# High parts of the weights moved to byte 96, loads in turns, and each half of stationary weights in two runs of four

## The chip, the cores and the metric

The kernel runs on one core of a Trainium2 chip, in one launch. The metric is the device time of that launch in microseconds, the median of several runs. All weights come from the chip's memory (HBM) once, some 317 MB, and are used once.

## The reference

The reference is two layers of an encoder over 256 positions of 2048 channels, in fp32, and a last RMSNorm. Each layer is a norm, one wide input projection, a mixer per group of heads, SiLU gates, one output projection of 4096 channels back to 2048, and the residual.

```
h = rms_norm(x, norm_w[0])                                   # layer 0
a_q, a_i, a_ff, a_fb, a_g, b_u, b_g = split(h @ w_in)        # 2048 -> 7 x 2048
a_out = hgrn2(a_q, a_i, a_ff, a_fb) * silu(a_g)              # gated linear recurrence, both directions
b_out = fourier(b_u) * silu(b_g)                             # 2-D DFT per group, linear map
x = x + concat(a_out, b_out) @ w_out
h = rms_norm(x, norm_w[1])                                   # layer 1
c_in, c_b, c_c, c_g, d_z, d_xbc, d_dt = split(h @ w_in)      # 2048 -> 13376
c_out = c_b * conv3(c_c * c_in) * silu(c_g)
d_out = ssd(d_xbc, d_dt, d_z)                                # scan in chunks, both directions
x = x + concat(c_out, d_out) @ w_out
return rms_norm(x, final_norm_w)
```

## The kernel before

Each fp32 operand is split into a high part (the value as TensorE's type fp32r holds it) and a low part (what is left). A product is then three products: high by high, high by low, low by high. TensorE's fp32r matmuls do these. The activations stand in `xx` (layer inputs, 16 blocks of 128 channels, each with its high and its low part of 256 positions behind one another) and in `mm` (inputs of the output projections).

The weights are worked off in halves: 561 tiles of 128 x 1024, in the order of use (`halves`, L105 to L112). SyncE's queue loads a half into one of five raw buffers (`load`, L125). ScalarE rounds it to its high part (L155), VectorE subtracts to get its low part (L156). Both go to a ring of three places (`fetch`, L133), up to four halves ahead of use (`half`, L175). The last eight halves have three more places.

There are three kinds of large matmul:
- Projections by channel (`gemm_half`, L184; 368 halves): the weights are stationary, eight blocks of 128 x 128 per half, and the activations move. Eight matmuls with the high weights take both parts of the activations (512 columns, L187), then eight with the low weights take the high activations (256 columns, L190).
- Token projections (`tokens`, L553, matmuls at L563; names pv and pg): the activations are stationary, the weights move, 512 columns. Twelve matmuls per half, eight with a high part moving and four with a low part.
- Output projections (`tproduct`, L198, matmuls at L206; names o, oC, oD): the inputs in `mm` are stationary, the weights move, 512 columns, twelve per half.

Where a tile begins in its partition is part of the change. Bytes are counted modulo 512 here. All steps between blocks of `xx`, `mm` and the weights are multiples of 512, so a tile has one place. `xx` begins at 480 (96 modulo 128; a spare tile `fx` of 120 floats puts it there), `mm` at 0. The ring's three places are 8704 bytes apart, 17 x 512. In projections and token projections the high part begins at 32 and the low part at 32; in output projections both begin at 0 (`oh, ol`, L146).

Small products (heads of the recurrence, Fourier groups, scan) are put between by `later(n, fn)` (L159): they are due n halves later, and `due` runs what is due before a half is taken, the earliest first and among those of one due time the one entered first. A scheduler then gives each engine its final order within what the tiles allow. The opening is written out at L301: it loads weight halves (w) and blocks of the activations (x) in the order `wxwxwwxwx`; the first weight half comes in two pieces.

Of the kernel before, what the change touches and what calls it, by code (L numbers as in the profile page):

```python
# [9 lines left out]
F32R = mybir.dt.float32r  # L10
# [5 lines left out]
P = 128  # L16
D = 2048
L = 256
# [38 lines left out]
def encoder_kernel(ctx: ExitStack, tc, xT, xN, w_ev, w_evo, w_dt, w_od, w_odo, fw, fnr, par, con, acon, tric, outN):  # L57
    nc = tc.nc
    V, S, PE = nc.vector, nc.scalar, nc.tensor
# [22 lines left out]
    def pcol(name, i):  # L82
        return parT[:, PCOL[name] + i:PCOL[name] + i + 1]
# [9 lines left out]
    def t2(name, shape=(2, L)):  # L93
        return lpool[0].tile([P, *shape], F32, tag="t2", name=name, bufs=N2)
# [16 lines left out]
    DTH = 2 * (112 + 32) + 1  # L111
    halves.insert(DTH, w_dt)  # L112

    moving = set(range(2 * 112, 2 * 144)) | set(range(len(halves) - 64, len(halves)))
    loaded, ready, waiting = {}, {}, []
    state = {"load": 0, "next": 0, "use": 0}
    HK = KT // 2
    NRAW, NHL, AHEAD = 5, 3, 4

    def pieces(n):  # L120
        return (slice(0, 512), slice(512, 1024)) if n == 0 else (slice(0, 1024),)
# [3 lines left out]
    def load():  # L125
        n = state["load"]
        state["load"] = n + 1
        raw = wpool.tile([P, HK * P], F32, tag=f"raw{n % NRAW}", name=f"raw{n}")
        for c in pieces(n):
            nc.sync.dma_start(out=raw[:, c], in_=halves[n][:, c])  # L130
        loaded[n] = raw

    def fetch():  # L133
        n = state["next"]
        state["next"] = n + 1
        if n >= state["load"]:
            load()
        raw = loaded.pop(n)
        kept = n - (len(halves) - 8)
        i = n % NHL if kept < 0 else kept % (2 * NHL)  # L140
        pool = wpool if i < NHL else endp[0]

        ring = i < NHL
        hi = pool.tile([P, HK * P + (8 if ring else 0)], F32R, tag=f"hi{i}", name=f"hi{n}")
        lo = pool.tile([P, HK * P + (120 if ring else 0)], F32R, tag=f"lo{i}", name=f"lo{n}")
        oh, ol = (0, 0) if not ring else (0, 120) if n in moving else (8, 0)  # L146
        hi, lo = hi[:, oh:oh + HK * P], lo[:, ol:ol + HK * P]
        if n == DTH:

            for i, w in enumerate((hi, lo)):  # L150
                w, r = w.rearrange("p (k s c) -> p k s c", s=2, c=64), raw.rearrange("p (i k c) -> p i k c", i=2, c=64)[:, i]
                S.activation(w[:, :, 0], r, AF.Copy)
                V.tensor_tensor(w[:, :, 1], r, w[:, :, 0].bitcast(F32), SUB)
        for c in pieces(n) if n != DTH else ():
            S.activation(hi[:, c], raw[:, c], AF.Copy)  # L155
            V.tensor_tensor(lo[:, c], raw[:, c], hi[:, c].bitcast(F32), SUB)  # L156
        ready[n] = (hi, lo)

    def later(n, fn):  # L159

        waiting.append((state["use"] + n, len(waiting), fn))

    def due(upto):
        while True:
            now = [w for w in waiting if w is not None and w[0] <= upto]
            if not now:
                return
            w = min(now)
            waiting[w[1]] = None
            w[2]()  # L170

    def flush():
        due(1 << 30)

    def half():  # L175

        n = state["use"]
        due(n)
        while state["next"] <= min(n + AHEAD, len(halves) - 1):
            fetch()  # L180
        state["use"] = n + 1
        return ready.pop(n)

    def gemm_half(out, a, k0, first, last):  # L184
        hi, lo = half()
        for k in range(HK):
            PE.matmul(out, lhsT=hi[:, k * P:(k + 1) * P], rhs=a[:, k0 + k].rearrange("p s n -> p (s n)"),  # L187
                      start=(first and k == 0), stop=False)
        for k in range(HK):
            PE.matmul(out[:, :L], lhsT=lo[:, k * P:(k + 1) * P], rhs=a[:, k0 + k, 0], start=False,  # L190
                      stop=(last and k == HK - 1))

    def gemm(out, a):

        for h in range(2):
            gemm_half(out, a, h * HK, h == 0, h == 1)
# [90 lines left out]
        PE.matmul(warm[:, :P], lhsT=ones, rhs=ones, start=True, stop=True)  # L287
    xcs = []

    def x_load():  # L290
        c = len(xcs)
        xc = t2(f"x{c}")
        for k in (slice(0, 1), slice(1, 2)) if c == 0 else (slice(0, 2),):
            nc.sync.dma_start(out=xc[:, k], in_=xT[:, 2 * c + k.start:2 * c + k.stop, :])
        xcs.append(xc)

    def x_split(c):
        for k in range(2):
            split_by(xx[:, 2 * c + k], xcs[c][:, k, :], pcol("nw0", 2 * c + k))

    for n in "wxwxwwxwx":  # L301
        (load if n == "w" else x_load)()
    for k in range(2):
        w, src = pcol("nw0", k), xcs[0][:, k, :]
        V.tensor_scalar(xx[:, k, 0], src, w, None, MUL)  # L305
        if k == 0:
            fetch()
        V.scalar_tensor_tensor(xx[:, k, 1], src, w, xx[:, k, 0].bitcast(F32), MUL, SUB)
    for c in (1, 2):
        fetch()  # L310
        x_split(c)
# [11 lines left out]
    def norm0b():  # L323
# [6 lines left out]
        rs["tok"] = rsqrt("n0t", pt[:, 0:2], 2)  # L330

    later(4, lambda: nc.sync.dma_start(out=parT[:, 16:], in_=par[:, 16:]))
    later(12, norm0)
    later(14, norm0b)


    with lay:
# [33 lines left out]
        def hgrn(h, q, Z, v, sg, vo):  # L371
# [94 lines left out]
                split_by(mm[:, h], pt.rearrange("p i n -> p (i n)"), pcol("hnw", h))  # L466


            later(6, scores)
            later(10 if h % 2 else 12, values)  # L470
            later(12 if h % 2 else 16, norm)

# [80 lines left out]
        def tokens(*names, each=lambda u: None):  # L553

            ps_ = [[pmain(f"{name}_{b}") for b in range(2)] for name in names]
            for u in range(8):
                each(u)
                for p in ps_:
                    hi, lo = half()
                    for k in range(2):  # L560
                        for b in range(2):
                            for n, (s_, w) in enumerate(((0, hi), (0, lo), (1, hi))):
                                PE.matmul(p[b], lhsT=xx[:, 2 * u + k, s_, b * P:(b + 1) * P],  # L563
                                          rhs=w[:, k * 4 * P:(k + 1) * 4 * P], start=(u == 0 and k == 0 and n == 0),
                                          stop=(u == 7 and k == 1 and n == 2))
            due(state["use"])
            return ps_

        def x_on(u):
            if 1 <= u < 6:  # L570
                x_split(u + 2)
            if u < 4:
                x_load()

        nrt = sp.tile([P, 2], F32, tag="nrt", name="nrt")
        for hp in range(8):
# [20 lines left out]
            for i in range(2):  # L597
                h = 2 * hp + i
                q = evac(f"q{h}", proj(f"pq{h}"))
                Z = t2(f"Z{h}")  # L600
                for d in range(2):
                    scaled(Z[:, d, :], f"Z{h}_{d}", proj(f"pz{h}_{d}"), rs[0])
                hgrn(h, q, Z, v, sg, (h % 4) * P)
# [18 lines left out]
    def tok(name, bufs=4):  # L622
        return op.tile([P, 4 * P], F32, tag="tok", name=name, bufs=bufs)
# [10 lines left out]
    for g in range(4):  # L634
# [7 lines left out]
        for b in range(2):  # L642
            V.tensor_tensor(x1[b], x1[b], po[b], ADD)
            nc.sync.dma_start(out=x1d[b, :, g * 4 * P:(g + 1) * 4 * P], in_=x1[b])
            s = tok(f"x1s{g}_{b}", 4)
# [4 lines left out]
    with ExitStack() as lay:  # L650
# [52 lines left out]
        H2 = 64  # L703
        dtp, first_b = pmain("pdt"), pmain("pB0")
        gemm_half(first_b, xx, 0, True, False)
        hl = half()
        due(state["use"])
        for k in range(KT):
            PE.matmul(dtp, lhsT=hl[k // HK][:, k % HK * P:(k % HK + 1) * P], rhs=xx[:, k].rearrange("p s n -> p (s n)"),
                      start=(k == 0), stop=(k == KT - 1))  # L710
        gemm_half(first_b, xx, HK, False, True)
        due(state["use"])
        xd, ee, rr, r2, dt, la, sc, rw = [t1(f"dt_{n}")[:H2] for n in ("x", "e", "r", "r2", "dt", "la", "sc", "rw")]
# [318 lines left out]
```

## Time and profile before

| | us |
|---|---|
| median of 3 runs (range) | 1670.77 (1670.48 to 1671.13) |
| profiled execution | 1671.18 |
| its span | 1669.4 |
| TensorE busy | 1656.1 |
| VectorE busy | 1236.5 |
| ScalarE busy | 935.8 |

The span is the time from the first to the last instruction; the profiled execution's own time also holds what lies around it. The page gives the busy time of each engine, the chain of work that ended last, and groups of instructions by line. Matmuls overlap: one lasts longer in the records than the distance to the next one's start, so their pace is read from starts. The chain of work shows it directly, since there a piece ends where the next one begins.

### The profile page before, as it was taken

How to read it: one execution, taken by the hardware profiler on the slowest of the kernel's cores; microseconds unless marked ns; L12 is line 12 of the kernel's file. 1: busy time of each engine (PE TensorE's matmuls, PEld its weight loads, DVE VectorE, ACT ScalarE, POOL GpSimd, SP SyncE). 2: the span in 40 equal slices, each digit the busy share in tenths (PEclk: the TensorE clock that was granted, in tenths of full speed). 3: DMA queues.
4: the chain of work that ended last, by engine and by line, in shares of the span. 5: the costliest groups of instructions: out<-in, count | busy, mean ns of one | idle time of the engine just before them, and what ended most of it. 6: DMA issues, size and time to landing. Idle time of an engine off the chain costs nothing.

```text
span 1669.4 us, 24942 instructions
## 1 busy us (share of the span) xinstructions
PE 1656.1 (99%) x9350; PEld 1412.3 (85%) x9350; DVE 1236.5 (74%) x2165; ACT 935.8 (56%) x1525; POOL 1.7 (0%) x12
## 2 busy tenths in 40 slices
PE   9999999999999999999999999999999999999997
PEld 7888888888888888888888888888888888888886
DVE  7788658875877589654458998888888798865554
ACT  6566456654665466544445666666655565654443
POOL 0000000000000000000000000000000000000000
PEclk9999999999999999999999999999999999999999
DMA  8654555455544654576665676656656665566553
GB/s 293 213 171 153 182 191 179 156 171 196 174 167 163 195 179 152 165 224 208 202 218 184 208 212 204 198 190 205 199 184 204 194 192 185 178 225 226 191 194 123
DMA packets 98265, 319.07 MB, mean 191 GB/s; under 512 B 11040, under 2 KB 19936, under 8 KB 98016
## 3 DMA queue, kind: packets, MB, share of 16 engines
q1 hardware_dynamic: 97712, 316.95, 57.9%
q8 instruction: 73, 1.20, 0.3%
q10 hardware_dynamic: 432, 0.53, 0.1%
q14 instruction: 48, 0.39, 0.1%
HBM read 313.18 MB, written 4.26 MB: 190 GB/s over the span
## 4 chain that ended last, share of the span: by engine, by line
PE 97%; DVE 1%; DMA 1%; ACT 0%; issue 0%; SPq 0%; DVEq 0%; ACTq 0%
PE pz L187 10%; PE o L206 10%; PE pg L563 5%; PE oC L206 5%; PE oD L206 5%; PE pz L190 5%; PE pv L563 5%; PE pu L187 4%; PE px L187 4%; PE pq L187 4%; PE pbg L187 4%; PE pcg L187 4%; PE pcb L187 3%; PE pci L187 3%; PE pcc L187 3%; PE pbg L190 2%
## 5 line engine op out<-in xcount | busy, mean ns | idle before, releaser
L156 DVE TENSOR_TENSOR lo<-raw,hi 128x1024 fp32r<-128x1024 f32 (+1 forms) x561 | 683.9, 1221 | 382.2 <-ACT hi L155 377.6
L155 ACT ACTIVATE hi<-raw 128x1024 fp32r<-128x1024 f32 (+1 forms) x561 | 594.3, 1060 | 565.1 <-PE o L206 86.0
L187 PE MATMUL pz<-xx,hi 128*128 128x512 f32 x768 | 194.9, 396 | 0.0
L187 PEld LDWEIGHTS pz<-xx,hi 128*128 128x128 f32 x768 | 137.2, 188 | 25.6
L206 PE MATMUL o<-hi,mm 128*128 128x512 f32 x512 | 126.8, 390 | 0.0
L206 PEld LDWEIGHTS o<-hi,mm 128*128 128x128 f32 x512 | 95.8, 188 | 19.7
L190 PEld LDWEIGHTS pz<-xx,lo 128*128 128x128 f32 x768 | 102.0, 188 | 8.7
L190 PE MATMUL pz<-xx,lo 128*128 128x256 f32 x768 | 103.3, 277 | 0.0
L563 PE MATMUL pv<-hi,xx 128*128 128x512 f32 x256 | 83.0, 394 | 0.8 <-DVE xx L305 0.8
L563 PE MATMUL pg<-hi,xx 128*128 128x512 f32 x256 | 81.6, 393 | 0.9 <-ACT hi L155 0.9
L206 PE MATMUL o<-lo,mm 128*128 128x512 f32 x256 | 68.5, 389 | 0.0
L187 PE MATMUL pcb<-xx,hi 128*128 128x512 f32 x256 | 66.4, 401 | 0.0
L187 PE MATMUL px<-xx,hi 128*128 128x512 f32 x256 | 66.0, 400 | 0.0
L187 PE MATMUL pu<-xx,hi 128*128 128x512 f32 x256 | 65.6, 398 | 0.0
L187 PE MATMUL pbg<-xx,hi 128*128 128x512 f32 x256 | 65.5, 398 | 0.0
L187 PE MATMUL pci<-xx,hi 128*128 128x512 f32 x256 | 65.4, 397 | 0.0
L187 PE MATMUL pq<-xx,hi 128*128 128x512 f32 x256 | 65.0, 395 | 0.0
L206 PE MATMUL oC<-hi,mm 128*128 128x512 f32 x256 | 64.7, 390 | 0.2 <-ACT hi L155 0.2
L187 PE MATMUL pcc<-xx,hi 128*128 128x512 f32 x256 | 64.8, 395 | 0.0
L187 PE MATMUL pcg<-xx,hi 128*128 128x512 f32 x256 | 64.8, 395 | 0.0
L206 PE MATMUL oD<-hi,mm 128*128 128x512 f32 x256 | 63.4, 390 | 0.0
L563 PEld LDWEIGHTS pg<-hi,xx 128*128 128x128 f32 x256 | 48.0, 188 | 11.7 <-ACT hi L155 1.3
(560 smaller groups left out, 2781.0 us busy)
## 6 DMA issues: line engine op xcount, KB each, us to landing
raw<-in_w_ev SPq DMA_DIRECT2D x223, 512.0 KB, 4.1
raw<-in_w_od SPq DMA_DIRECT2D x208, 512.0 KB, 4.4
raw<-in_w_evo SPq DMA_DIRECT2D x64, 512.0 KB, 4.0
raw<-in_w_odo SPq DMA_DIRECT2D x64, 512.0 KB, 4.5
ab<-rd SPq DMA_DIRECT2D x64, 128.0 KB, 4.9
fw<-in_fw SPq DMA_DIRECT2D x8, 256.0 KB, 5.7
xr<-in_xN SPq DMA_DIRECT2D x8, 256.0 KB, 5.9
x1d<-xr SPq DMA_DIRECT2D x8, 256.0 KB, 4.9
```

Of the source, the lines that this page charges most:

```text
L155: S.activation(hi[:, c], raw[:, c], AF.Copy)
L156: V.tensor_tensor(lo[:, c], raw[:, c], hi[:, c].bitcast(F32), SUB)
L187: PE.matmul(out, lhsT=hi[:, k * P:(k + 1) * P], rhs=a[:, k0 + k].rearrange("p s n -> p (s n)"), start=(first and k == 0), stop=False)
L190: PE.matmul(out[:, :L], lhsT=lo[:, k * P:(k + 1) * P], rhs=a[:, k0 + k, 0], start=False, stop=(last and k == HK - 1))
L206: PE.matmul(outs[b], lhsT=a[:, k0 + 2 * u + k, s_, b * P:(b + 1) * P], rhs=w2[part][:, k * 4 * P:(k + 1) * 4 * P], start=(u == 0 and part ...
L563: PE.matmul(p[b], lhsT=xx[:, 2 * u + k, s_, b * P:(b + 1) * P], rhs=w[:, k * 4 * P:(k + 1) * 4 * P], start=(u == 0 and k == 0 and n == 0), ...
```

## The change

The diff has four parts.

1. In each ring place the low part is now allocated first and has 8 spare floats, the high part behind it has 120. In the projections by channel the high part begins at 96 modulo 512 (`PLACES`, 16 floats behind a place of 32), the low part stays at 32. In output projections both stay at 0. In token projections (`passing`) the high part begins at 32, 96 or 480 by ring place, the low part at 32.
2. `gemm_half` goes through its eight blocks in two runs: four matmuls with high weights, four with low, four with high, four with low.
3. The two pieces of the first weight half and the two of the first activations are loaded in turns.
4. `later` takes a second key: the scores of every second head go behind whatever else is due at the same half.

```
+    PLACES = (16, 16, 16)
...
+        for i, c in enumerate(pieces(n)):
             nc.sync.dma_start(out=raw[:, c], in_=halves[n][:, c])
+            if n == 0:
+                x_load(i)
...
-        hi = pool.tile([P, HK * P + (8 if ring else 0)], F32R, tag=f"hi{i}", name=f"hi{n}")
-        lo = pool.tile([P, HK * P + (120 if ring else 0)], F32R, tag=f"lo{i}", name=f"lo{n}")
-        oh, ol = (0, 0) if not ring else (0, 120) if n in moving else (8, 0)
+        lo = pool.tile([P, HK * P + (8 if ring else 0)], F32R, tag=f"lo{i}", name=f"lo{n}")
+        hi = pool.tile([P, HK * P + (120 if ring else 0)], F32R, tag=f"hi{i}", name=f"hi{n}")
+        oh, ol = (0, 0) if not ring else (120, 0) if n in moving else ((0, 16, 112)[i] if n in passing else PLACES[i], 8)
...
-    def later(n, fn):
-        waiting.append((state["use"] + n, len(waiting), fn))
+    def later(n, fn, last=0):
+        waiting.append((state["use"] + n, last, len(waiting), fn))
...
-        for k in range(HK):
-            PE.matmul(out, lhsT=hi[:, k * P:(k + 1) * P], rhs=a[:, k0 + k].rearrange("p s n -> p (s n)"),
-                      start=(first and k == 0), stop=False)
-        for k in range(HK):
-            PE.matmul(out[:, :L], lhsT=lo[:, k * P:(k + 1) * P], rhs=a[:, k0 + k, 0], start=False,
-                      stop=(last and k == HK - 1))
+        for ks in (range(HK // 2), range(HK // 2, HK)):
+            for k in ks:
+                PE.matmul(out, lhsT=hi[:, k * P:(k + 1) * P], rhs=a[:, k0 + k].rearrange("p s n -> p (s n)"),
+                          start=(first and k == 0), stop=False)
+            for k in ks:
+                PE.matmul(out[:, :L], lhsT=lo[:, k * P:(k + 1) * P], rhs=a[:, k0 + k, 0], start=False,
+                          stop=(last and k == HK - 1))
...
-            later(6, scores)
+            later(6, scores, h % 2)
```

On TensorE, the projections of the first Fourier group (pu) stand like this before, two of them:

```order
L187 MATMUL pu_0_925<-xx,hi_793 128x512 x8
L190 MATMUL pu_0_925<-xx,lo_794 128x256 x8
L187 MATMUL pu_0_925<-xx,hi_815 128x512 x8
L190 MATMUL pu_0_925<-xx,lo_816 128x256 x8
L187 MATMUL pu_1_994<-xx,hi_842 128x512 x8
```

and now, of one and a half:

```order
L198 MATMUL pu_1_994<-xx,hi_843 128x512 x4
L201 MATMUL pu_1_994<-xx,lo_842 128x256 x4
L198 MATMUL pu_1_994<-xx,hi_843 128x512 x4
L201 MATMUL pu_1_994<-xx,lo_842 128x256 x4
L198 MATMUL pu_1_994<-xx,hi_865 128x512 x4
L201 MATMUL pu_1_994<-xx,lo_864 128x256 x4
```

Each run of eight became two of four, with the low run between them. The output tile and the number of matmuls are the same.

On TensorE, between the two gate projections (pbg) of that group, before (sa and sb are a head's scores, po its values, fp the Fourier products over channels):

```order
L449 MATMUL po_1115<-v_528,ST_947 128x128 x4
L425 MATMUL sa_1128<-DQ_912,D_900 64x64 x2
L425 MATMUL sa_1128<-q_1_917,k_1_918 64x64 x2
L425 MATMUL sa_1128<-DQ_912,D_900 64x64 x4
L425 MATMUL sa_1128<-q_1_917,k_1_918 64x64 x2
L425 MATMUL sa_1128<-DQ_912,D_900 64x64 x2
L431 MATMUL sb_1129<-q_1_919,k_1_920 64x128 x4
L507 MATMUL fp_1152<-acT,F_1055 128x128 x4
L187 MATMUL pbg_1_1114<-xx,hi_997 128x512 x8
```

and now:

```order
L461 MATMUL po_1115<-v_528,ST_947 128x128 x4
L198 MATMUL pbg_1_1114<-xx,hi_998 128x512
L519 MATMUL fp_1128<-acT,F_1055 128x128
L437 MATMUL sa_1136<-DQ_912,D_900 64x64
L519 MATMUL fp_1128<-acT,F_1055 128x128 x3
L437 MATMUL sa_1136<-DQ_912,D_900 64x64
L437 MATMUL sa_1136<-q_1_917,k_1_918 64x64 x2
L437 MATMUL sa_1136<-DQ_912,D_900 64x64 x4
L437 MATMUL sa_1136<-q_1_917,k_1_918 64x64 x2
L437 MATMUL sa_1136<-DQ_912,D_900 64x64 x2
L443 MATMUL sb_1137<-q_1_919,k_1_920 64x128 x4
L198 MATMUL pbg_1_1114<-xx,hi_998 128x512 x3
```

One large matmul moved up behind the values, and the Fourier products went ahead of or between the first scores; all the same instructions are there. The same happens in six groups.

On SyncE's queue, the opening before (raw is a weight half or a piece of one, x a block of activations):

```order
L130 DMA raw_102<-in_w_ev 128x512 x2
L294 DMA x_105<-in_xT 128x256 x2
L130 DMA raw_108<-in_w_ev 128x1024
L294 DMA x_110<-in_xT 128x512
L130 DMA raw_112<-in_w_ev 128x1024
L130 DMA raw_114<-in_w_ev 128x1024
L294 DMA x_116<-in_xT 128x512
```

and now:

```order
L138 DMA raw_102<-in_w_ev 128x512
L305 DMA x_104<-in_xT 128x256
L138 DMA raw_102<-in_w_ev 128x512
L305 DMA x_104<-in_xT 128x256
L138 DMA raw_108<-in_w_ev 128x1024
L305 DMA x_110<-in_xT 128x512
L138 DMA raw_112<-in_w_ev 128x1024
L138 DMA raw_114<-in_w_ev 128x1024
```

The first two transfers of each kind stand in turns; from the second weight half on the order is the same.

## Rows read from the trace of the kernel before

**Rows 1.** The page: busy us, share, instructions; granted TensorE clock in tenths, 40 slices.

```profile
PE 1656.1 (99%) x9350; PEld 1412.3 (85%) x9350; DVE 1236.5 (74%) x2165; ACT 935.8 (56%) x1525; POOL 1.7 (0%) x12
...
PEclk9999999999999999999999999999999999999999
```

**Rows 2.** TensorE's waits, whole span: us in total, times, longest.

```profile
PE warm L287 <- DVE epsT L283: 1.1, 1, 1.1
PE pg L563 <- ACT hi L155: 0.9, 1, 0.9
PE pv L563 <- DVE xx L305: 0.8, 1, 0.8
PE pt L465 <- DVE on L458: 0.5, 1, 0.5
PE pg L563 <- DVE lo L156: 0.5, 1, 0.5
PE py L805 <- DVE e L798: 0.4, 1, 0.4
PE oC L206 <- ACT hi L155: 0.2, 1, 0.2
```

**Rows 3.** The chain of work, 240 to 252 us: start us, us, what.

```profile
239.87 0.93 PE pz L187 x4
...
241.71 1.86 PE pq L187 x8
243.57 0.91 PE pq L190 x8
...
250.03 1.86 PE pz L187 x8
```

**Rows 4.** The chain of work, whole span, its longest pieces.

```profile
203.09 21.98 PE pg L563 x96
...
1000.05 2.07 PE px L187 x8
...
1507.49 21.76 PE oC L206 x96
```

**Rows 5.** Busy time of high-part projection matmuls (L187), whole span: TensorE, weight loads.

```profile
0.00:1670.00 1670.00, 751.31 (x2944) 526.64 (x2944) 1.00 0.58 191
```

**Rows 6.** The chain of work, 900.9 to 903 us.

```profile
901.42 0.86 PE cb L844 x4
```

**Rows 7.** The page: groups of the token projections' high parts: busy us, mean ns.

```profile
L563 PE MATMUL pv<-hi,xx 128*128 128x512 f32 x256 | 83.0, 394 | 0.8 <-DVE xx L305 0.8
L563 PE MATMUL pg<-hi,xx 128*128 128x512 f32 x256 | 81.6, 393 | 0.9 <-ACT hi L155 0.9
```

**Rows 8.** The timeline, 98.8 to 99.4 us: VectorE, then TensorE.

```profile
98.64 1.22 DVE L156 TENSOR_TENSOR lo<-raw,hi 128x1024 fp32r<-128x1024 f32 x1
...
99.05 0.62 PE L187 MATMUL pbg<-xx,hi 128*128 128x512 f32 x2
```

**Rows 9.** The chain of work, 104 to 109 us.

```profile
108.03 1.16 PE pbg L187 x5
```

**Rows 10.** The timeline, 0 to 16 us.

```profile
6.25 0.47 PE L563 MATMUL pv<-hi,xx 128*128 128x512 f32 x1 [0.85 <-DVE xx L305]
```

**Rows 11.** The chain of work, 0 to 16 us.

```profile
2.59 6.45 DMA raw<-in_w_ev
...
9.06 1.06 ACT hi L155
...
10.15 1.24 DVE lo L156
...
11.43 2.56 PE pg L563 x10
```

**Rows 12.** The chain of work, 696.9 to 698 us.

```profile
696.83 0.46 PE pbg L190 x4
697.29 0.93 PE o L206 x4
```

More of the change, by code (lines that the diff above doesn't have):

```diff
@@ L112, in encoder_kernel @@
     halves.insert(DTH, w_dt)
+    PLACES = (16, 16, 16)
+    passing, n = set(), 0
+    for hp in range(8):
+        if hp % 2 == 0:
+            passing |= set(range(n, n + 16))
+            n += 16
+        n += 12 + (8 if hp < 6 else 0 if hp == 6 else 16)
     moving = set(range(2 * 112, 2 * 144)) | set(range(len(halves) - 64, len(halves)))
@@ L128, in load @@
         raw = wpool.tile([P, HK * P], F32, tag=f"raw{n % NRAW}", name=f"raw{n}")
-        for c in pieces(n):
+        for i, c in enumerate(pieces(n)):
             nc.sync.dma_start(out=raw[:, c], in_=halves[n][:, c])
+            if n == 0:
+                x_load(i)
         loaded[n] = raw
@@ L168, in due @@
             w = min(now)
-            waiting[w[1]] = None
-            w[2]()
+            waiting[w[2]] = None
+            w[3]()
     def flush():
@@ L288, in encoder_kernel, with x_load @@
     xcs = []
[L290 to L295, printed above, removed]
+    def x_load(piece=None):
+        c = len(xcs) if not piece else 0
+        xc = xcs[0] if piece else t2(f"x{c}")
+        k = slice(0, 2) if piece is None else slice(piece, piece + 1)
+        nc.sync.dma_start(out=xc[:, k], in_=xT[:, 2 * c + k.start:2 * c + k.stop, :])
+        if not piece:
+            xcs.append(xc)
     def x_split(c):
@@ L299, in x_split @@
             split_by(xx[:, 2 * c + k], xcs[c][:, k, :], pcol("nw0", 2 * c + k))
-    for n in "wxwxwwxwx":
+    for n in "wwxwwxwx":
         (load if n == "w" else x_load)()
```

## The prediction

> **What bounds the kernel now.** I read the page's busy shares first, then TensorE's waits, then the chain of work that ended last, and at last single stretches of that chain. TensorE is busy for 1656.1 of 1669.4 us, and its granted clock is in the top tenth in all 40 slices, so this is the 2.4 GHz level throughout [rows 1]. Its waits add up to 4.4 us, and the reader is to see there that after the warm-up the two longest, 0.9 and 0.8 us, belong to the first token projections, and that no other is over 0.5 [rows 2]. So neither ScalarE, VectorE nor the loads hold this kernel back: its time is the number of matmuls times the pace at which they follow each other, and a change can win only through that pace, or lose through it or through a new wait.
>
> The pace is read from starts in the chain. In a projection (activations move, weights are stationary) eight high-part matmuls take 1.86 us and eight low-part ones 0.91; from 241.71 to 250.03 three halves pass, 2.773 us each [rows 3]. With 0.91 for the low parts, a high-part matmul of 512 columns takes (2.773 - 0.91) / 8 = 232.9 ns. The output projections run the same shape, 96 in 21.76 us, or 226.7 ns, and the token projections 96 in 21.98 us, or 229.0 ns [rows 4]. Three paces for one shape, at one clock: what differs is where the operands begin. Modulo 128 bytes the output projections have both operands at 0 (equal places). The projections have the weights at 32 and the activations at 96, the token projections the activations at 96 and the weights at 32 (64 bytes apart in both). I read that as: operands 64 bytes apart cost 2 to 6 ns per matmul, equal places cost nothing. It is the simplest reading of three rows, not a proven rule.
>
> **The change part by part.** *High parts at 96.* In the projections the high weights now begin at 96, as the activations do. 2944 matmuls stand at that line [rows 5]. If all came to 226.7 ns, they would give 2944 x 6.2 = 18.3 us. The low parts stay at 32. While a high-part matmul streams, TensorE loads the weights of the matmul behind it, so the last of each run streams beside a low part's load, and the two places differ by 64 bytes there as before. With two runs per half this is 2 of 8 (it would be 1 of 8 in one run). I take 6 of 8: 2208 x 6.2 = 13.7 us. The trace of before has no equal places at 96, so this is bounded from both sides by the nearest rows: at best the 215 ns per pass (0.86 us for four) of the fp32 products with 256 columns, the fastest large passes in the chain [rows 6], 2944 x 17.9 = 52.7 us less; at worst one more step of the size seen, 232.9 + 6.2 = 239.1 ns, 18.3 us more. I take 226.7 because it is the row of the same shape and type with equal places.
>
> By the Trainium skill (TensorE: Matmul & The Clock Gate, step-by-step part on what each phase is for) TensorE reads its moving and its stationary operand through two independent ports, and loading the next weights takes nothing from the running matmul. By that rule no place could matter and this term would be zero. The rows above, three paces for one shape, do not agree with it as far as they go, but they don't show that the place is the cause.
>
> *Token projections.* Their high weights now lie at 32, 96 or 480 by ring place, so two of three are at 96 modulo 128, equal to the activations. 512 of their matmuls move a high part [rows 7]; two thirds, 341, by at most 2.3 ns is 0.8 us less. It could as well cost that much; I take the 0.8 less, by the same reading.
>
> *Two runs of four.* At the old places this costs nothing: four high parts take 0.93 us [rows 3], half of the 1.86 for eight, and a half with its one change from high to low and back costs no more than its sixteen matmuls. The order within the half does ask for the first low part after four matmuls instead of eight, 0.93 us sooner. Low parts are otherwise ready microseconds ahead, but not in eight halves of layer 0, of which one is shown: VectorE ends that low part at 98.64 + 1.22 = 99.86, and the half's matmuls begin at 99.05 [rows 8]. The new first use is at 99.98, and its weight load starts one matmul earlier, at 99.75. That is a wait of 0.1 us, 8 x 0.1 = 0.9 us at most with rounding; behind it on TensorE stands the rest of the half, and nobody else waits. I count 0.9. The high buffer is now released by the eighth high matmul at 2.3 us into the half instead of 1.9; the next use of that ring place is two halves (5.5 us) later, and the rounding to it takes about 1 us on ScalarE and 1.2 on VectorE, so this is covered.
>
> *Scores after what else is due.* In six groups one projection matmul now stands between the small products of a head, and the Fourier products come between the score products. Each is one more return from small to large matmuls. Such a return is seen at most in the 2.07 us of eight after a small product against 1.86 [rows 3, 4]; six times 0.21 is 1.3 us as the upper end, and 108.03 shows five in 1.16 us, no loss, as the lower one [rows 9]. I take 0.3.
>
> *Loads in turns.* The first activations come after the first half of the first weight tile instead of after both. TensorE's first real matmul, which waited for VectorE's split of them until 6.25 [rows 10], can start earlier, by up to 0.8. But the second weight tile lands at 9.04 behind the same bytes as before, and from there ScalarE at 9.06 and VectorE at 10.15 set the matmul at 11.43 [rows 11]. The wait that goes comes back at that one, so I count 0; were that load sooner too, it would be 0.8 us less.
>
> **Sum.** The profiled execution took 1671.18 us, its span 1669.4 plus 1.8 around it, 0.4 above the median of 1670.77. 1671.2 - 13.7 - 0.8 + 0.9 + 0.3 - 0 = 1657.9, so 1658 us.
>
> **The rivals.**
> *A run of four never settles (no change).* The first four matmuls of the output projection, right behind a projection, take 0.93 us [rows 12], 232.5 ns each, though the same line later runs at 226.7. If every run of four starts that way after its low parts, nothing of the 13.7 us arrives, and the ends meet at 1671.2 - 0.8 + 1.2 = 1671.6 us. For it: exactly the row, and that runs are now half as long. Against it: the half of today shows no slow start, its last four take 0.93 of the 1.86. 0.14.
>
> *The place doesn't count (no change).* The three paces would then come from what the stages differ in besides, the order of operands or the buffers written, and only the small terms move: 1671.2 + 1.2 = 1672.4 us. For it: no stage of before shows one loop at two places. Against it: the projections and the output projections both run one weight after the other. 0.05. It is what the ports of the page named above, of the Trainium skill, would make of the change.
>
> *The new place is worse (slower).* If what counts is not the difference modulo 128 but the place itself, or the distance modulo 256 or 512, 96 against 480 may cost one step more: 239.1 ns, 1671.2 + 18.3 + 1.2 = 1691 us; half a step gives 1681. It decides as soon as a high-part matmul takes over 234.0 ns, since 1.1 x 2944 is 3.3 us. For it: token projections and projections have the same distance modulo 128 and still differ by 3.9 ns, so modulo 128 is not the whole of it. Against it: the one row with equal places is the fastest. 0.25.
>
> *All eight gain, or more.* If the load beside a matmul doesn't count, only its own operands, all of 18.3 us come: 1653. This belongs to my forecast's side and range. Down to 215 ns it would be 1619; nothing of this type runs that fast here, 0.06.
>
> **How the numbers follow.** Forecast (6 or 8 of 8 gain) 0.50, its own range 1650 to 1664. No change 0.14 + 0.05 = 0.19, worse place 0.25, far faster 0.06. The range of 8 in 10 reaches from 1648, leaving out the far faster case and some of the forecast's lower end, to 1682, leaving out the full step of the slower case. 0.2% is 3.3 us, about what a measurement of this kernel tells from no change: faster 0.56, same 0.19, slower 0.25.
>
> **What would show it.** In the changed profile's chain, four high parts should take 0.91 us in place of 0.93 and a half about 2.73 in place of 2.773. The low parts should stay at 0.91 for eight (0.455 for four), and the output projections at 21.76 for 96. Busy time at the line of the high parts should fall by about 14 us with 2944 as before. TensorE's waits should gain small ones for low parts, and the wait for the first activations should go while the one for the next low part stays. The forecast is wrong if four high parts still take 0.93, or if low parts slow down beside high loads at 96.

## The result, and the profile after

The changed kernel takes 1681.88 us (median of four runs, 1680.96 to 1683.36) against 1670.95 for the kernel before: ratio 1.0067, 95% interval 1.0051 to 1.0083, so 11 us slower. The forecast was 13 us faster. The time lies just inside the upper end of the range, 1682, and the chance of slower had been put at 0.25.

The page of the kernel after, busy us, share and instructions, then the granted clock in 40 slices; it answers to [rows 1]:

```profile
PE 1664.2 (99%) x9350; PEld 1421.2 (85%) x9350; DVE 1237.9 (74%) x2165; ACT 934.2 (56%) x1525; POOL 1.7 (0%) x12
...
PEclk9999999999999999999999999999999999999999
```

The number of matmuls and the clock are as before, and TensorE is again busy for all but 15 us of its span of 1679.2. "99% busy" says nothing here of where 10 us went: the records of successive matmuls overlap by some 0.15 us, and a late start first takes up that overlap before it shows as idle time. Nor does the busy time of the high-part projections tell anything; its row answers to [rows 5] (the busy time of TensorE and of the weight loads, each with its count):

```profile
0.00:1680.00 1680.00, 806.74 (x2944) 500.55 (x2944) 1.00 0.58 190
```

It rose by 55 us where the kernel lost 11, because each of the 368 halves now has one run more, whose last matmul is on record to its end beside the next run's start, 0.15 us each. Only starts tell the pace. Three successive halves of the kernel after in layer 1, on TensorE's timeline (start, us, line, tile, count), answer to [rows 3]:

```profile
1081.39 1.08 PE L198 MATMUL pcg<-xx,hi 128*128 128x512 f32 x4
1082.31 0.62 PE L201 MATMUL pcg<-xx,lo 128*128 128x256 f32 x4
1082.78 1.08 PE L198 MATMUL pcg<-xx,hi 128*128 128x512 f32 x4
1083.70 0.62 PE L201 MATMUL pcg<-xx,lo 128*128 128x256 f32 x4
1084.16 1.08 PE L198 MATMUL pcg<-xx,hi 128*128 128x512 f32 x4
```

Four high parts take 0.92 us, four low ones 0.47, a half 1084.16 - 1081.39 = 2.77 us. That is the pace of before to the hundredth. From start to start and matmul by matmul (medians over the halves), the eight high parts took 1863 ns before and take 1844 now, the eight low ones 910 and 930: by their starts the high parts gained, and the low parts gave it back.

Where the time went is read from two tiles: `pB` opens layer 1, `oD` its output projection. Their tile views, of before and then of after (after the count: shortest, median and longest ns, first and last start):

```profile
L187 PE MATMUL pB<-xx,hi x16: 393/396/398, 874.0 to 883.0; 128*128 128x512 f32 x16
...
L206 PE MATMUL oD<-hi,mm x44: 387/389/504, 1484.7 to 1499.8; 128*128 128x512 f32 x44
```

```profile
L198 PE MATMUL pB<-xx,hi x16: 387/392/396, 883.4 to 892.9; 128*128 128x512 f32 x16
...
L217 PE MATMUL oD<-hi,mm x16: 387/389/504, 1494.4 to 1498.8; 128*128 128x512 f32 x16
```

From `pB` to `oD` it is 610.7 us before and 611.0 after; `pB` comes 9.4 us late. All but 0.3 us of the loss lies in layer 0. There the sum over the distances from each matmul's start to the next, by tile, has grown most at the gates `pbg` (high 3.95 us, low 0.9), at the Fourier products `fp` (2.4) and at the scores `sa` (1.0).

TensorE's waits of the kernel after (us in total, times, longest) answer to [rows 2]:

```profile
PE pbg L201 <- DVE lo L166: 1.3, 6, 0.3
...
PE pg L575 <- DVE lo L166: 0.5, 1, 0.5
PE pg L575 <- ACT hi L165: 0.5, 1, 0.5
PE fp L519 <- DVE F L509: 0.4, 1, 0.4
...
PE pz L201 <- DVE lo L166: 0.2, 1, 0.2
```

New are waits for a low part in layer 0, six times at the gates and once in `pz`, and that of `fp` for VectorE's `F`. One is gone, the first token projection for `xx`. Its opening on the timeline answers to [rows 10, 11]:

```profile
5.76 0.48 PE L575 MATMUL pv<-hi,xx 128*128 128x512 f32 x1
...
9.26 0.73 PE L575 MATMUL pg<-hi,xx 128*128 128x512 f32 x2 [0.50 <-ACT hi L165]
10.52 0.50 PE L575 MATMUL pg<-lo,xx 128*128 128x512 f32 x1 [0.53 <-DVE lo L166]
```

The first real matmul starts 0.49 us sooner, and the one for the second low part, which had stood at 11.43, 0.91 sooner.

### The profile page after: what moved, and what is told of

It reads as the page before. It is cut to its first block, busy times and chain, and to the rows that moved or that the text cites. A ratio compares the mean times of both kernels' runs of the same rounds, so it can differ in the third digit from the quotient of the medians.

```text
span 1679.2 us, 24926 instructions
## 1 busy us (share of the span) xinstructions
PE 1664.2 (99%) x9350; PEld 1421.2 (85%) x9350; DVE 1237.9 (74%) x2165; ACT 934.2 (56%) x1525; POOL 1.7 (0%) x12
## 5 line engine op out<-in xcount | busy, mean ns | idle before, releaser
L198 PE MATMUL pz<-xx,hi 128*128 128x512 f32 x768 | 209.0, 394 | 0.0
L198 PEld LDWEIGHTS pz<-xx,hi 128*128 128x128 f32 x768 | 130.3, 188 | 15.7
L201 PEld LDWEIGHTS pz<-xx,lo 128*128 128x128 f32 x768 | 117.8, 189 | 17.1 <-DVE lo L166 0.6
L201 PE MATMUL pz<-xx,lo 128*128 128x256 f32 x768 | 120.1, 278 | 0.2 <-DVE lo L166 0.2
L198 PE MATMUL pbg<-xx,hi 128*128 128x512 f32 x256 | 71.8, 399 | 0.0
L198 PE MATMUL pcb<-xx,hi 128*128 128x512 f32 x256 | 71.1, 399 | 0.0
L198 PE MATMUL pu<-xx,hi 128*128 128x512 f32 x256 | 70.3, 396 | 0.0
L198 PE MATMUL pci<-xx,hi 128*128 128x512 f32 x256 | 70.1, 396 | 0.0
L198 PE MATMUL pcc<-xx,hi 128*128 128x512 f32 x256 | 69.4, 393 | 0.0
L198 PE MATMUL pcg<-xx,hi 128*128 128x512 f32 x256 | 69.4, 393 | 0.0
```

## The experiments

Each kernel was timed beside the kernel before; ratios are to that, with their 95% interval. "Half" is the time of the sixteen matmuls of an undisturbed projection half, from start to start.

### Taking the change apart

Three kernels add one part to the kernel before, one takes the key out of the kernel after.

```
e1_no_key     (after)    -  later(6, scores, h % 2)      +  later(6, scores)
e2_key_only   (before)   -  later(6, scores)             +  later(6, scores, h % 2)   with the second key of `later`
e3_places     (before)   +  PLACES, passing, order and spare floats of lo and hi as in the change
e4_runs       (before)   -  for k in range(HK): hi; for k in range(HK): lo
                         +  for ks in (range(HK // 2), range(HK // 2, HK)): four hi, four lo
```

> The changed kernel with the scores of every second head back at the same rank as the rest (later without its second key). Theory K (the second key is what costs: in six groups of layer 0 the large and small products of pbg, fp and sa change places one by one, 1.4 us a group in the trace of after): about 8 us come back, 1672 to 1674 us, and the Fourier products fp take 7.2 us in all again instead of 9.6. Rival W (the loss is the low parts asked for sooner, and small waits that follow in the same places): the order of the small products goes back but the time stays at 1680 us or more.

> The kernel before with the second key alone. Theory K: slower by 7 to 9 us, 1678 to 1680 us, with the layer 1 part unchanged. Rival W: no slower than 1672 us, since runs of eight ask for no low part sooner.

> The kernel before with the places of the weights alone (high parts at 96 in the projections; runs of eight). Theory P0 (the place of the stationary weights does not set the pace): 2.773 us per half as before and 1671 us. Rival P1 (equal places do help, and the runs of four took the gain away, so that both cancelled in after): a half takes 2.73 us or less and the time is 1653 to 1660 us. Rival P2 (the places cost and the runs gave it back): over 2.80 us per half, over 1680 us.

> The kernel before with the two runs of four alone, at the old places. Theory P0: 2.773 us per half, and 0 to 2 us more in all from low parts that are asked for 0.93 us sooner in eight halves, 1671 to 1673 us. Rival P1: a half takes 2.82 us, about 1688 us. Rival P2: a half takes 2.73 us, about 1656 us.

Measured: e1_no_key 1676.38 us, 1.0037 [1.0025, 1.0050]; e2_key_only 1675.15, 1.0030 [1.0019, 1.0041]; e3_places 1673.64, 1.0020 [1.0011, 1.0030]; e4_runs 1675.10, 1.0028 [1.0017, 1.0039]; before 1670.41. Every one of the three parts costs by itself: key 4.7 us, runs 4.7, places 3.2. Together, 12.6 us, they are more than the whole loss, so none of them needs another to do harm. Without the key the changed kernel takes 1681.88 - 1676.38 = 5.5 us less. No expectation had the sizes right: by the theories put first, the key was to cost 7 to 9 us, the runs of four at most 2, the places nothing.

### The runs of four: the release of the high buffer

Theory R: what comes late is not the demand but the supply. ScalarE's rounding into a ring place waits for the last high matmul that uses it, VectorE's subtraction waits for that rounding, and VectorE's queue behind is worked off in order. The rival: the low part is merely asked 0.93 us sooner. Two other orders within the half were to tell them apart. f1_low_early asks the first low part as soon as the change does but releases the high buffer almost as before; f2_high_last asks it almost as before and releases last.

```
f1_low_early:  high 0..3, low 0, high 4..7, low 1..7
f2_high_last:  high 0..6, low 0..7, high 7
```

> The kernel before, with one low-part matmul of each half moved up behind the fourth high one (4 high, 1 low, 4 high, 7 low). The low part is asked for 0.93 us sooner, as in two runs of four, but the high buffer is released only 0.11 us later instead of 0.46. Theory R (in the runs of four the later release of the high buffer delays ScalarE's next rounding and with it VectorE's queue, and that makes the low part late in eight halves): 0.1 to 0.3 us in each of eight halves, 1 to 2.5 us in all, 1671.5 to 1673 us. Rival S (asking sooner is all of it): 0.5 us in each as in the runs of four, 1674 to 1676 us.

> The kernel before, with the eight low matmuls of each half put ahead of the eighth high one (7 high, 8 low, 1 high). The high buffer is released 0.91 us later, the low part is asked for only 0.23 us sooner. Theory R: low parts come 0.9 us later in the eight gate halves, at 1.7 us into the half where they are wanted at 1.4 to 1.6: waits of 0.2 to 0.4 us each, 2 to 3.5 us in all, 1672.5 to 1674 us. Rival S: no wait, since low parts were ready 0.8 us into the half: 1670 to 1671 us.

Measured: f1_low_early 1671.65, 1.0006 [0.9996, 1.0015]; f2_high_last 1675.17, 1.0027 [1.0016, 1.0038]; before 1670.45. Asking early costs 1.2 us, and the interval holds 1. f2_high_last is as slow as e4_runs, but it doesn't bear out R: its trace has no wait for a low part at the gates. The order on VectorE changed there, and the gate's low part comes sooner than before. Its timeline at the gate of [rows 8]:

```profile
98.00 1.20 DVE L156 TENSOR_TENSOR lo<-raw,hi 128x1024 fp32r<-128x1024 f32 x1
...
98.89 1.80 PE L187 MATMUL pbg<-xx,hi 128*128 128x512 f32 x7
```

It ends 0.31 us into the half where R expected 1.7, and these gate halves take 2.773 us, as undisturbed ones do. f2_high_last loses elsewhere, 2.4 of the 3.7 us of its trace in layer 1; why is not shown.

The mechanism stands in the other timelines. Of the kernel before, TensorE and ScalarE some 13 us ahead of the gate of [rows 8] (start, us, engine, line, tile, count, idle time before it):

```profile
85.55 1.07 PE L190 MATMUL pz<-xx,lo 128*128 128x256 f32 x8
...
85.75 1.06 ACT L155 ACTIVATE hi<-raw 128x1024 fp32r<-128x1024 f32 x1 [1.44 <-PE pz L187]
```

The same of the kernel after, and 13 us later its first two runs of the gate with VectorE's low part between:

```profile
85.44 0.62 PE L201 MATMUL pz<-xx,lo 128*128 128x256 f32 x4
...
85.64 1.06 ACT L165 ACTIVATE hi<-raw 128x1024 fp32r<-128x1024 f32 x1 [1.44 <-PE pz L198]
...
98.50 1.09 PE L198 MATMUL pbg<-xx,hi 128*128 128x512 f32 x4
98.52 1.22 DVE L166 TENSOR_TENSOR lo<-raw,hi 128x1024 fp32r<-128x1024 f32 x1
...
99.79 0.73 PE L201 MATMUL pbg<-xx,lo 128*128 128x256 f32 x4 [0.20 <-DVE lo L166]
100.36 1.08 PE L198 MATMUL pbg<-xx,hi 128*128 128x512 f32 x4
```

In both, the rounding waited for the last high matmul and starts 0.20 us after the last low run has begun. From it to VectorE's subtraction for the gate it is 98.64 - 85.75 = 12.89 us before [rows 8] and 98.52 - 85.64 = 12.88 after: a fixed chain through both engines. From the end of that half to the gate TensorE needs 99.05 - (85.55 + 0.91) = 12.59 before and 98.50 - (85.44 + 0.46) = 12.60 after. What differs is the first link: the release comes 0.71 us ahead of the half's end with eight low matmuls behind it, and 0.26 with four. So the low part ends 0.81 us into the gate's half before and 1.24 after, where it is wanted at 0.93. The half's first run takes 1.29 us in place of 0.92, the low run behind it 0.57 in place of 0.46, and 0.5 us is lost in all. Eight halves of e4_runs (six gates, one of `pz`, one of `pu`) lose 0.40 to 0.55 us each, 4.0 together; its trace is 3.6 us longer than that of before, its median 4.7. f1_low_early, first the end of the earlier half, then the same gate:

```profile
85.31 0.96 PE L191 MATMUL pz<-xx,lo 128*128 128x256 f32 x7
...
85.50 1.06 ACT L155 ACTIVATE hi<-raw 128x1024 fp32r<-128x1024 f32 x1 [1.44 <-PE pz L187]
...
98.40 3.49 DVE L156 TENSOR_TENSOR lo<-raw,hi 128x1024 fp32r<-128x1024 f32 x3
98.69 1.09 PE L187 MATMUL pbg<-xx,hi 128*128 128x512 f32 x4
99.66 0.39 PE L191 MATMUL pbg<-xx,lo 128*128 128x256 f32 x1
```

With 0.80 us for seven low matmuls, the release comes 85.31 + 0.80 - 85.50 = 0.61 us ahead of the half's end, and the low part ends 98.40 + 1.22 - 98.69 = 0.93 us into the gate's half, where it is asked at the same moment. So three kernels release 0.71, 0.61 and 0.26 us ahead and have the low part at 0.81, 0.93 and 1.24: each tenth by which the release is late comes back 13 us behind. The six gate halves of f1_low_early lose 0.17 to 0.21 us each. R holds for the runs of four, on these three.

### The second key: products that wait for VectorE

Theory F: the key puts the Fourier products `fp` ahead of the scores, at a time when VectorE has not yet made their input `F`; and they need not stand there. Then to enter them one half later takes the cost away and leaves the key in.

```
f3_key_channels3 (e2_key_only)   -  later(2, channels)      +  later(3, channels)
```

> The kernel before with the second key, and the Fourier products over channels due one half later (3 instead of 2), so that they no longer come ahead of the scores. Theory F (with the key alone TensorE waits for VectorE's F, the input of these products, 0.4 us in six groups, and changes shapes around it): the 4.7 us go, 1670 to 1671.5 us. Rival G (the key costs through the scores themselves, which come later and hold up what waits for them): 1674 us or more.

Measured: 1670.52, 1.0000 [0.9991, 1.0010]; before 1670.45. The cost is gone. But the scores of f3_key_channels3 stand directly behind `po` again, so the run alone doesn't part F from G; the trace of e2_key_only does. First TensorE in e2_key_only between two gates, and its wait in the list of waits (total, times, longest):

```profile
169.04 1.05 PE L449 MATMUL po<-v,ST 128*128 128x128 f32 x8
170.50 1.27 PE L507 MATMUL fp<-acT,F 128*128 128x128 f32 x8 [0.40 <-DVE F L497]
171.70 0.34 PE L425 MATMUL sa<-DQ,D 128*64 128x64 f32 x4
...
172.44 0.61 PE L431 MATMUL sb<-q,k 128*64 128x128 f32 x8
172.98 1.90 PE L187 MATMUL pbg<-xx,hi 128*128 128x512 f32 x7
```

```profile
PE fp L507 <- DVE F L497: 2.6, 7, 0.4
```

and the same place in the kernel before, where the scores stand first:

```profile
168.50 1.05 PE L449 MATMUL po<-v,ST 128*128 128x128 f32 x8
169.48 0.34 PE L425 MATMUL sa<-DQ,D 128*64 128x64 f32 x4
...
170.77 1.16 PE L507 MATMUL fp<-acT,F 128*128 128x128 f32 x8
171.68 2.10 PE L187 MATMUL pbg<-xx,hi 128*128 128x512 f32 x8
```

From `po` to the gate the same small products take 172.98 - 169.04 = 3.94 us instead of 171.68 - 168.50 = 3.18, 0.76 more, and six such groups are 4.6 of the 4.7 us. The first step, from `po`, is 1.46 instead of 0.98: 0.48 with the wait in it. The rest, 0.29, is in `fp` itself, from its first matmul to the next product: 1.20 us behind a wait and ahead of scores, 0.91 behind scores and ahead of the gate; the views don't tell which end of it counts. Over layer 0 of e2_key_only the distances from start to start grew by 3.07 us at `po` and 1.92 at `fp`, and at no other tile by more than 0.6, so nothing behind the scores was held up, as G would have it. Before, the scores had covered VectorE's work on `F`. The kernel after pays the same in another form, one large matmul and single scores scattered between:

```profile
169.74 1.05 PE L461 MATMUL po<-v,ST 128*128 128x128 f32 x8
170.55 0.47 PE L198 MATMUL pbg<-xx,hi 128*128 128x512 f32 x1
171.08 0.49 PE L519 MATMUL fp<-acT,F 128*128 128x128 f32 x2
171.50 0.33 PE L437 MATMUL sa<-DQ,D 128*64 128x64 f32 x2
171.76 0.94 PE L519 MATMUL fp<-acT,F 128*128 128x128 f32 x6
...
173.91 0.96 PE L198 MATMUL pbg<-xx,hi 128*128 128x512 f32 x3
```

Without the one large matmul (0.23) that is again 173.91 - 169.74 - 0.23 = 3.94 us. The list of waits shows 0.4 us of it once; the rest hides in distances that no wait is put down to.

### The places

f4_all_at_0 puts activations, high and low parts at byte 0 (equal places everywhere, as in the output projections), and the three g kernels move the low parts of the projections from there. h3_places_proj is e3_places with the token projections at their old places.

```
f4_all_at_0     xx 480 -> 0;  oh, ol -> 0 for every half
g1, g2, g3      as f4_all_at_0, low part of the projections by channel at 32, 64, 96
h3_places_proj  (e3_places)  -  (0, 16, 112)[i] if n in passing   +  0 if n in passing
```

> The kernel before with all operands of large matmuls at 0 modulo 512: activations xx moved from 480 to 0, high and low weights from 32 to 0 in projections and token projections too. Theory E (equal places at a round address give the pace of the output projections): a high-part matmul 226.7 ns, a half 2.72 us, about 1650 us. Rival N (the pace of a projection does not come from places): 2.773 us per half, 1670 to 1672 us. Rival B (places at 0 are worse for the low parts of 256 columns): over 2.80 us per half, 1680 us or more.

> The kernel before with activations xx, high parts and all moving weights at 0 modulo 512, but the low parts of the projections at 32. In the run with all at 0 a high matmul came down to 227 ns after five of each run and the low ones went up from 113 to 120 ns. Theory L (the low parts' 120 comes from low weights and activations at one place): low back to 113 ns, high as in that run, a half 1841 + 907 = 2748 ns, 368 x 25 = 9 us less, and token projections at 2.720 us per half, 1.7 us less: 1659 to 1661 us. Rival M (the 120 comes from the place of the activations alone): 1673 to 1675 us as with all at 0.

> As the run with the low parts at 32, with the low parts of the projections at 64. Theory L: 1659 to 1661 us here too if any other place than 0 will do. Rival M: 1673 to 1675 us. A time between would say that each distance has its own price.

> As the run with the low parts at 32, with the low parts of the projections at 96. Theory L: 1659 to 1661 us. Rival M: 1673 to 1675 us.

> The places of the change in the projections by channel alone: their high weights begin at 96, those of the token projections stay at 32 in all three ring places, runs of eight, all else as before. With the places in both kinds the loss was 3.2 us. If the token projections carry their share (twelve token matmuls 2787 and 2770 ns at 96 and 480 instead of 2747, worked out as 1.35 us), the loss here is 1.9 us and all token halves come back to 2747 ns. If the price sits in the projections by channel alone (halves of 2780 ns instead of 2773, 368 x 7 ns = 2.6 us), the loss stays at 2.6 to 3.2 us.

Measured, with the places modulo 512 as activations / high / low of the projections by channel, the half, and twelve token matmuls:

| kernel | places | half, ns | 12 token matmuls, ns | us | ratio |
|---|---|---|---|---|---|
| before | 480 / 32 / 32 | 2773 | 2747 | | |
| e3_places | 480 / 96 / 32 | 2780 | 2758, 2787, 2775 (high at 32, 96, 480) | 1673.64 | 1.0020 [1.0011, 1.0030] |
| h3_places_proj | 480 / 96 / 32 | 2780 | 2747 | 1671.92 | 1.0006 [0.9997, 1.0015] |
| f4_all_at_0 | 0 / 0 / 0 | 2793 | 2720 | 1674.43 | 1.0026 [1.0015, 1.0036] |
| g1_low_32 | 0 / 0 / 32 | 2803 | 2720 | 1674.44 | 1.0021 [1.0012, 1.0031] |
| g2_low_64 | 0 / 0 / 64 | 2780 | 2720 | 1670.03 | 0.9994 [0.9985, 1.0004] |
| g3_low_96 | 0 / 0 / 96 | 2806 | 2720 | 1675.08 | 1.0025 [1.0015, 1.0035] |

The chain of work of f4_all_at_0 (start, us, what), a projection's two halves and a token projection, which answer to [rows 3, 4]:

```profile
241.31 1.84 PE pq L186 x8
243.15 0.95 PE pq L189 x8
244.10 1.84 PE pq L186 x8
...
202.82 21.76 PE pg L562 x96
```

and of e3_places, token projections of the opening, and a stretch of 96:

```profile
13.63 2.79 PE pv L571 x12
...
24.80 2.75 PE pv L571 x12
...
203.43 22.19 PE pg L571 x96
```

Three things follow. The place counts: the same loop, clock and shape takes 21.76, 21.98 [rows 4] or 22.19 us per 96 with nothing changed but where tiles begin. Equal places modulo 128 are not what counts: token matmuls with the high weights at 96 or 480 beside activations at 480 are slower (2787 and 2775 ns per twelve) than with weights at 32 (2747). Nor are a matmul's own operands all of it: in e3_places the token halves with weights at 32, as before, take 2758 ns between halves at 96 and 480. And what one kind of matmul gains, another gives back: with all at 0 the high run falls from 1.86 to 1.84 us, but the low run rises from 0.91 to 0.95. The low parts were to tell whether their own place (L) or the activations' (M) sets that; with the activations at 0 no place of the low parts brought 0.91 back, which speaks for M, but the halves still range from 2780 to 2806 ns, so the low part's place counts as well. For f4_all_at_0 none of E, N and B came out. Which property of the addresses does it stays open.

h3_places_proj splits the price: with the token projections at their old places all of them run at 2747 ns again, and 1.46 us is left of 3.2 (its own interval holds 1). The difference, 1.8, is near the 1.35 us by which the distances of the token matmuls have grown in the trace of e3_places; the timings alone don't part them, since the intervals touch. The 1.46 belong to halves of 2780 ns in runs of eight. In the change's runs of four the half is 2773 again, so there they are not seen.

### Loads in turns, and the version the runs point to

```
t1_turns        (before)      the loads in turns of the change, alone
h4_low64_turns  (g2_low_64)   the same on top
```

> The kernel before with the loads in turns alone. Theory O (the trace of after passes the opening 0.6 us sooner and keeps that): 0.3 to 0.8 us less, 1669.7 to 1670.2 us. Rival Z (my prediction: the second weight tile lands when it did, so the gain of the first matmul is waited away): within 0.2 us of before.

> The one arrangement of places that was no slower than before (activations and all high parts at 0, low parts of the projections at 64, 0.7 us faster in its one comparison), with the loads in turns on top, runs of eight, no second key. If the two are independent, 0.7 + 0.2 to 0.55 us come together: 1669.5 us, ratio 0.9992. If the difference of the places was noise of that comparison, 1670.4 us. Either way the first real matmul starts near 5.7 us instead of 6.25 and token halves take 2720 ns.

Measured: t1_turns 1670.57, 0.9997 [0.9987, 1.0006]; h4_low64_turns 1669.70, 0.9994 [0.9985, 1.0002]. In the trace of t1_turns the opening comes 0.55 us sooner and the distance is kept to the end, but the timing can't tell that from nothing. h4_low64_turns has the lowest median of all, 0.8 us under its kernel before, and its interval holds 1. So the one part of the change worth keeping is worth about half a microsecond, and no place tried gives more than that.

## Why the prediction was wrong

**High parts at 96 (-13.7 us; measured: no gain).** The step that failed, in the largest term, is "operands 64 bytes apart cost 2 to 6 ns per matmul, equal places cost nothing". It was drawn from three rows of three different loops. Its first half, that places count, is shown by the runs. Its rule for which ones is refuted: equal places at 96 gave a half of 2780 ns in runs of eight, 7 more than before. With the change's runs of four, four high parts take 922 ns against 929 at the old places (e4_runs), and four low ones 465 against 457. The prediction's last sentence had named this way to fail, low parts that slow down beside high parts at 96, but gave it no price and no chance. "6 of 8" failed too: with high parts and activations both at 0 only the last three of eight come near 226.7.

From the Trainium skill (TensorE: Matmul & The Clock Gate, step-by-step part), by which the two operands come through independent read ports, the prediction drew a rule by which no place could matter, and gave it 0.05. The page itself says nothing of places. The runs refute the rule so drawn: the same 96 matmuls take 21.76, 21.98 and 22.19 us at different places. The rival built on it expected 1672.4 us, from unchanged pace; the pace of a half did come out unchanged, but as two changes that cancel.

**Token projections (-0.8; +1.35 in the trace).** The same rule, with the wrong sign.

**Two runs of four (+0.9; measured +4.7).** The eight halves of layer 0 were right, and so was the new wait for the low part; its size, 0.1 us each, was not (0.40 to 0.55). Wrong was the sentence "the next use of that ring place is two halves (5.5 us) later ... so this is covered". The next use of the buffer is covered, but the release also starts the rounding, and with it everything that VectorE does in order behind it; the low part came 0.43 us later, on top of being asked 0.93 us sooner. The idle 1.44 us in front of ScalarE's rounding, put down to TensorE's high matmuls, stood in the trace of before and was not read. Where a releaser is named, moving the release moves the chain.

**Second key (+0.3; measured +4.7).** The term priced a return from small to large matmuls, 0 to 0.21 us. It did not ask what the products that come forward wait for. VectorE made the first piece of `F` at this place of the kernel before in this row (start, us, tile, count):

```profile
169.49 0.42 DVE L497 TENSOR_TENSOR F<-U 128x256 f32<-128x256 f32 x1
```

It ends at 169.91, and the new order wants it where the scores had begun, at 169.48: 0.43 us late, the size of the wait that came. The upper end of 1.3 us was too low because it was taken from the wrong kind of row.

**Loads in turns (0; about -0.5 in the trace).** "The second weight tile lands at 9.04 behind the same bytes as before" was wrong: in the kernel after the matmul that stood at 11.43 starts at 10.52, and with the loads in turns alone at 10.86. There the second weight tile lands at 8.47 instead of 9.04, though the same bytes stand ahead of it.

**Sum.** 4.7 + 4.7 + 3.2 - 0.2 = 12.4 us by the single parts (of the loads in turns the timed 0.2), against 10.9 measured for the whole; without the 1.46 of the places that runs of four don't pay it is 10.9. That fits, but the interval of each part is 1.6 to 1.8 us wide to either side. The rival "the new place is worse" had the right sign with the wrong mechanism, since at 96 the high matmuls stay under its 234.0 ns on average; no rival held the two mechanisms that decided, a late release and an input not yet made. That 1681.88 still lies inside the range is luck: its upper end, 1682, had been made for slower high matmuls, which did not come.

## What to carry to other kernels

When an order of work is changed, follow two things for every moved instruction: which engine's next step its end releases, and whether its inputs exist at the new time, by the clock of the engine that makes them. A kernel whose bound engine is 99% busy with hardly a wait is not safe from either: its margins can be 0.1 us wide in a few places, and a reorder that is free in 360 halves can lose half a microsecond in each of eight. A rule on addresses read from different loops is a guess until one loop has run at two places.

## What was not expected of the hardware

- The pace of one matmul shape at one clock depends on where the operands begin: 128x512 token matmuls 226.7, 229.0 or 232 ns, low-part 128x256 matmuls, as a rule, 113 ns with activations at 480 (before) and 120 with all at 0 (f4_all_at_0).
- Within an undisturbed run the distances follow a fixed pattern that repeats from half to half, as 226, 236, 231, 236, 231, 236, 231, 236 before; an average hides it.
- What a place gives one kind of matmul it can take from the next: high parts at 96 made four of them 7 ns faster and the four low ones behind them 8 ns slower, with the low parts' own place unchanged.
